# A gated pooling and convolution block on one core: a denser start, with dummy matrix products, wide transposes of the meta tokens and the first block of x in halves

## The chip, the cores and the metric

The kernel runs on one core of a Trainium2 chip. A core has a matrix engine (TensorE, PE in the profile), VectorE (DVE), ScalarE (ACT), GpSimd (POOL) and SyncE (SP). SP, ACT and POOL issue transfers (DMAs) from their own instruction queues, and each engine takes its instructions strictly in their order; an instruction that waits holds up everything behind it on that engine. The metric is the time of one execution on the device in microseconds; the median of several runs counts.

## The reference

One decoder layer over 16 learned meta tokens and 256 tokens of width 2048, in float32:

```python
h = jnp.concatenate([meta_b, x], axis=1)            # 16 + 256 tokens
u = rms_norm(h, g_pre_mix[l])
proj = u @ w_in[l]                                  # 2048 x 7168
z_pool, v_conv, g_conv, gate_a, gate_b = jnp.split(proj, splits, axis=-1)
y_a = causal_multiscale_pool(z_pool, w_pool_grp[l], pool_scale[l]) @ w_pool_out[l]
y_b = conformer_conv(v_conv, g_conv, w_dw[l], b_dw[l], conv_ln_g[l], conv_ln_b[l]) @ w_conv_out[l]
m = jax.nn.sigmoid(gate_a) * y_a + jax.nn.sigmoid(gate_b) * y_b
h = h + rms_norm(m @ w_o[l], g_post_mix[l])
u = rms_norm(h, g_pre_mlp[l])
f = jnp.square(jax.nn.relu(u @ w_up[l])) @ w_down[l]
h = h + rms_norm(f, g_post_mlp[l])
return h[:, N_META:]
```

The split has widths 1024, 1024, 1024, 2048 and 2048; the feed-forward width is 8192.

## The kernel before

Every large product is made of float32 numbers that are split in two parts, hi (rounded to the format fp32r) and lo (the rest), and runs as three products of parts: hi with the activations' hi, hi with their lo, lo with their hi. Weights stream in from memory in chunks of 1 MB, in the order in which they are used (`stream`); SP issues them, ACT casts each chunk to hi (line 250), VectorE subtracts to get lo (line 253), TensorE multiplies. The activations stand with channels on the partitions and tokens along the row (272 of them, the 16 meta tokens first), so x and meta have to be transposed first.

The change lies wholly in the first stage, the first 256 columns of v_conv. There the weights come as two chunks of eight k tiles each (a k tile is 128 input channels), and each k tile is a piece of 128x256 that is cast and split by itself. The order of the work, as it is written by hand (the scheduler is off):

- `make_identity` on GpSimd writes `ident`, the identity with which TensorE transposes.
- The transfers (lines 323 to 334): the meta tokens as 16 rows of 2048 (`m_in`, SP), the gain g_pre_mix (ACT), the first block of x, 512 columns, its lower 128 tokens on SP and its upper 128 on ACT, then the first chunk of weights as pieces of 1, 1, 2, 2 and 2 k tiles (the first on ACT, the rest on SP), block 1 of x (ACT), block 2 (SP), the second chunk, block 3.
- ACT then loads a function table and warms it (`warm_up`, line 286); `keep_warm(8)` puts eight dummy transposes of `ident` on TensorE (line 343).
- `meta_tokens` (lines 351 to 361): sixteen transposes of 16x128 from `m_in`, a transpose of the gain's rows into the columns `vecs` (lines 312 and 313), then VectorE multiplies by the gain (`mg`), ACT casts the hi part into `u`, VectorE makes the lo part. Four more dummies follow.
- `x_tile(k)` (lines 366 to 374): two transposes of 128x128 into one bank, ACT scales by the gain into the hi part of `u`, VectorE makes the lo part.
- The loop over k from -4 to 15: in its first four turns an x tile and a piece of weights each; from k = 0 on the six products of a k tile (`mm3`, line 422: two columns of 128, three products each), and after every odd k the next two x tiles. So the queue of TensorE is: four x tiles, the products of k = 0 and 1, x tiles 4 and 5, the products of k = 2 and 3, and so on.

`m_in` is also read much later, for the sums of squares of the meta tokens (`sq_tile`). `rb` is a tile that is written for the first time near 45 us, with the roots of these sums. Transfers of SP and ACT take one of eight completion semaphores in turn: the ninth transfer takes the first one's and waits, on its own queue, until the first has landed.

Of the kernel before, what the change touches and what calls it, by code (L numbers as in the profile page):

```python
# [8 lines left out]
F32 = mybir.dt.float32  # L9
# [5 lines left out]
P = 128  # L15
CK = 4
CW = 512
# [83 lines left out]
def hybrid_block(ctx: ExitStack, tc: tile.TileContext, ins: dict, out: bass.AP):  # L101
    nc = tc.nc
    x = ins["x"][0]
    meta = ins["meta"]
    T, D = x.shape
    M = meta.shape[0]
    L = M + T
    NT = T // P
    KD = D // P
# [17 lines left out]
    const = ctx.enter_context(tc.tile_pool(name="const", bufs=1))  # L127
# [3 lines left out]
    tmp = ctx.enter_context(tc.tile_pool(name="tmp", bufs=2))  # L131
# [3 lines left out]
    def f32(ap):  # L135
        return ap.bitcast(F32)

    def acc_tile(name):
        return psA.tile([P, CW], F32, tag="acc", name=name)

    def misc_tile(name):
        return psB.tile([P, CW], F32, tag="misc", name=name)
# [43 lines left out]
    HALF = (2 * CK, CW // 2)  # L186
# [24 lines left out]
    opened = []  # L211
# [13 lines left out]
    def part_tile(tag, n, standing=False):  # L225

        key = f"{tag}{n % 3}"
        room = ready.pop(key) if key in ready else part_room(key, f"{tag}_{n}")
        place = 2 if standing and tag == "hi" else 1
        shift = (place - 1 - 3 * KEYS.index(key)) % 4 * LINE  # L230
        return room[:, shift:shift + CK * CW]

    def open_chunk(first=((2, nc.sync),) * 4):
        n = at["n"]
        at["n"] += 1
        src, (rows, width) = stream[n]
        raw = raws.tile([P, CK * CW], F32, tag="raw", name=f"raw_{n}")
        hi, lo = (part_tile(tag, at["parts"], n in standing_chunks) for tag in ("hi", "lo"))
        at["parts"] += 1
        flat, (raw, hi, lo) = raw, (t.rearrange("p (k c) -> p k c", k=rows) for t in (raw, hi, lo))  # L240
        pieces = rows if n < FIRST + 1 else 1
        k = rows // pieces
        i = 0
        for n_, queue in first if n < FIRST else ((rows, nc.sync),):
            sl = slice(i, i + n_)
            queue.dma_start(raw[:, sl, :], src[:, sl, :])
            i += n_

        def high(sl):
            nc.scalar.copy(hi[:, sl, :], raw[:, sl, :])  # L250

        def low(sl):
            nc.vector.tensor_sub(lo[:, sl, :], raw[:, sl, :], f32(hi[:, sl, :]))  # L253

        def piece(i):
            def f():
                sl = slice(i * k, (i + 1) * k)
                high(sl)
                low(sl)
            return f  # L260
        opened.append((hi, lo, [piece(i) for i in range(pieces)], flat))
# [5 lines left out]
    def fetch(ahead=2):  # L267

        for c in range(ahead + 1):
            if c == len(opened) and at["n"] < len(stream):  # L270
                open_chunk()
            if c < len(opened):
                split_pieces(c)
        flush()
        return opened.pop(0)[:2]


    ident = const.tile([P, P], F32, name="ident")
    make_identity(nc, ident)
    ones = const.tile([P, P], F32, name="ones")  # L280
# [9 lines left out]
    m_in = big.tile([M, D], F32, tag="a", name="m_in")  # L290
# [9 lines left out]
    def load_rows(queue, *names):  # L300
        rows = tmp.tile([48, P], F32, tag="g", name=f"rows_{names[0]}")
        n = 0
        for name in names:
            v = ins[name][0].rearrange("(k p) -> k p", p=P)
            queue.dma_start(rows[n:n + v.shape[0], :], v)
            n += v.shape[0]
        return rows, n, names[0]

    def rows_to_columns(rows, n, name):

        pv = misc_tile(f"pv_{name}")
        nc.tensor.transpose(pv[:, :n], rows[:n, :], ident[:n, :n])
        nc.vector.tensor_copy(vecs[:, cols[name]:cols[name] + n], pv[:, :n])
# [1 line left out]
    def col(name, k):  # L315
        return vecs[:, cols[name] + k:cols[name] + k + 1]

    def load_x(queue, b, ts=slice(0, NT)):
        sl = slice(b * CW, (b + 1) * CW)
        queue.dma_start(x_in[:, ts, sl], xv[:, ts, sl])  # L320


    nc.sync.dma_start(m_in, meta)
    pre_rows = load_rows(nc.scalar, "g_pre_mix")
    for t, queue in enumerate((nc.sync, nc.scalar)):
        load_x(queue, 0, slice(t, t + 1))
    open_chunk(((1, nc.scalar), (1, nc.sync), (2, nc.sync), (2, nc.sync), (2, nc.sync)))
    load_x(nc.scalar, 1)
    load_x(nc.sync, 2)
    open_chunk()  # L330
    load_x(nc.sync, 3)
    other_rows = load_rows(nc.gpsimd, "pool_scale", "b_dw", "conv_ln_g", "conv_ln_b", "g_pre_mlp")
# [6 lines left out]
    idle = misc_tile("idle")  # L339

    def keep_warm(n):
        for _ in range(n):
            nc.tensor.transpose(idle[:, :P], ident, ident)

    keep_warm(8)

    u = big.tile([P, KD, 2, -(-L // (4 * LINE)) * 4 * LINE], F32R, tag="um", name="u")[:, :, :, :L]

    def meta_tokens():

        pt = acc_tile("xm")[:, :KD * M].rearrange("p (k m) -> p k m", k=KD)
        for k in range(KD):
            nc.tensor.transpose(pt[:, k, :], m_in[:, k * P:(k + 1) * P], ident[:M, :M])
        rows_to_columns(*pre_rows)
        mg = tmp.tile([P, KD, M], F32, tag="v", bufs=5, name="mg")
        g = vecs[:, cols["g_pre_mix"]:cols["g_pre_mix"] + KD]
        nc.vector.tensor_mul(mg, pt, g[:, :, None].broadcast_to([P, KD, M]))
        nc.scalar.copy(u[:, :, 0, :M], mg)  # L360
        nc.vector.tensor_sub(u[:, :, 1, :M], mg, f32(u[:, :, 0, :M]))

    meta_tokens()
    keep_warm(4)

    def x_tile(k):
        pt = acc_tile(f"xt_{k}")[:, :T]
        sl = slice(k * P, (k + 1) * P)
        for t in range(NT):
            nc.tensor.transpose(pt[:, t * P:(t + 1) * P], x_in[:, t, sl], ident)  # L370
        nc.scalar.activation(u[:, k, 0, M:], pt, AF.Copy, scale=col("g_pre_mix", k))
        nc.vector.scalar_tensor_tensor(
            u[:, k, 1, M:], pt, col("g_pre_mix", k), f32(u[:, k, 0, M:]),
            op0=ALU.mult, op1=ALU.subtract)

    def sq_tile(b, t):
        sl = slice(b * CW, (b + 1) * CW)
        junk = tmp.tile([P, CW], F32, tag="junk", bufs=1, name=f"sqx_{b}_{t}")
        src, n = (x_in[:, t, sl], P) if t < NT else (m_in[:, sl], M)
        nc.scalar.activation(junk[:n, :], src, AF.Square, accum_out=ssq[:n, t, b:b + 1])  # L380
# [6 lines left out]
        nc.vector.tensor_scalar(q, q, -0.5, 1.5, op0=ALU.mult, op1=ALU.add)  # L387
        nc.vector.tensor_mul(r, r, q)

    rb = const.tile([P, L], F32, name="rb")  # L390
    sc = {}

    def scale_roots():
# [23 lines left out]
    def mm3(acc, hi, lo, act, k, cs, first, last):  # L417


        off = act.shape[3] - acc.shape[1]  # L420
        for n, (w, a) in enumerate(((hi, 0), (hi, 1), (lo, 0))):
            nc.tensor.matmul(acc, w[:, k[0], cs], act[:, k[1], a, off:],  # L422
                             start=first and n == 0, stop=last and n == 2)
# [18 lines left out]
    def acc_tiles(name, n=CW // P):  # L442
        return [acc_tile(f"acc_{name}_{j}") for j in range(n)]
# [68 lines left out]
    def pieces_to(n):  # L512

        while first["split"] < min(n, (FIRST + 1) * HALF[0]):
            c = first["split"] // HALF[0]
            if c == at["n"]:
                open_chunk()
            opened[c][2].pop(0)()
            first["split"] += 1

    first = {"split": 0}
    accs = [acc[:, :L] for acc in acc_tiles("v0", HALF_CW // P)]
    squares = [(b, t) for b in range(XB) for t in range(NT + 1)]
    LEAD = 4
    for k in range(-LEAD, KD):
        if k < 0:
            x_tile(k + LEAD)

        pieces_to(min(k + LEAD + 1, KD) + 2 * max(k - KD + LEAD + 1, 0))
        if k < 0:  # L530
            continue
        if k >= HALF[0] and k % 2:
            sq_tile(*squares.pop(0))
        for j, acc in enumerate(accs):
            mm3(acc, *opened[k // HALF[0]][:2], u, (k % HALF[0], k), slice(j * P, (j + 1) * P),
                k == 0, k == KD - 1)
        if k % 2:
            for kx in range(k + LEAD - 1, min(k + LEAD + 1, KD)):
                x_tile(kx)
# [183 lines left out]
    for g in range(NG):  # L723
        for j in range(GK):
            q = g * GK + j
            acc = (acc_tile if q < KP - 2 else misc_tile)(f"acc_grp_{q}")[:, :T]
# [48 lines left out]
    for n in range(NB):  # L775
# [4 lines left out]
    m = big.tile([P, LINE + KD * 2 * T], F32R, tag="um", name="m")[:, LINE:].rearrange(  # L780
        "p (k a t) -> p k a t", k=KD, a=2)
# [421 lines left out]
    accs = acc_tiles("up00")  # L1203
# [498 lines left out]
    for e, cs in enumerate(col_halves):  # L1702
        for w, s in ends:
            h = AT[s][0]
# [47 lines left out]
```

## Time and profile before

| | us |
|---|---|
| median of 3 runs | 1208.12 |
| lowest and highest run | 1207.67, 1209.48 |
| the profiled execution, its own time | 1208.15 |
| its span, first to last instruction | 1206.4 |

The profiled execution stands 0.03 us above the median; its span leaves 1.75 us of its own time outside. The granted clock of TensorE is 0.998 of full speed as a mean. A row of the timeline gives the start and the length in microseconds, the engine (PEld is the loading of weights into TensorE, and a q behind an engine's name is its instruction queue issuing a transfer), the line, the operation, output and inputs, the shape and how many of them were merged into the row; in brackets the idle time ahead of it and what ended that.

### The profile page before, as it was taken

To read this page: it belongs to the slowest core of one execution; us is meant where nothing else is said; L and a number is where in the kernel's file an instruction comes from. 1 tells how busy PE (TensorE), PEld (TensorE's weight loads), DVE (VectorE), ACT (ScalarE), POOL (GpSimd) and SP (SyncE) were. 2 spreads that over 40 slices of the span, in tenths; PEclk is the share of its full clock that TensorE was granted. 3 is DMA by queue.
4 is the path that set the end of the run, shared out by engine and by line. 5 is a ranking of instruction groups with operands and counts; after the bars stand their busy time and mean duration, and the time that the engine had idled before them with its cause. 6 is when DMAs were issued, how large, how long until landed. Compare 5 with 4: busy or idle time off the path is not lost.

```text
span 1206.4 us, 15712 instructions
## 1 busy us (share of the span) xinstructions
PE 1195.8 (99%) x6444; PEld 1038.4 (86%) x6444; DVE 974.7 (81%) x1058; ACT 627.6 (52%) x651; POOL 8.3 (1%) x19
## 2 busy tenths in 40 slices
PE   9999999999999999999999999999999999999997
PEld 9999988888888888898888888888888888888886
DVE  6799978999776778688988878778878778888756
ACT  7533344443583454665555564564554555555542
POOL 1000000000000000000000000000000000000000
PEclk9999999999999999999999999999999999999999
DMA  9655555656558578546475674674764764755841
GB/s 289 210 175 175 178 202 180 208 177 207 175 169 280 176 256 262 181 160 221 144 244 174 187 232 158 198 249 141 245 199 156 261 200 149 244 175 178 275 141 70
DMA packets 162038, 238.27 MB, mean 198 GB/s; under 512 B 4033, under 2 KB 91521, under 8 KB 161440
## 3 DMA queue, kind: packets, MB, share of 16 engines
q1 hardware_dynamic: 159120, 229.98, 58.2%
q0 software_dynamic: 1680, 5.40, 1.7%
q10 hardware_dynamic: 1168, 1.91, 0.4%
q8 instruction: 50, 0.82, 0.3%
q14 instruction: 20, 0.16, 0.0%
HBM read 235.17 MB, written 2.10 MB: 197 GB/s over the span
## 4 chain that ended last, share of the span: by engine, by line
PE 99%; DVE 0%; DMA 0%; DVEq 0%; ACT 0%; issue 0%; ACTq 0%
PE bank_u L427 18%; PE acc_gate L682 14%; PE acc_up L1516 14%; PE bank_u L433 9%; PE bank_a L1516 7%; PE o_c L1020 6%; PE bank_b L1516 5%; PE acc_v L422 4%; PE acc_z L422 4%; PE acc_g L422 4%; PE acc_co L682 4%; PE acc_po L682 4%; PE acc_up L427 1%; PE bank_u L1516 1%; PE o_a L1020 1%; PE acc_up L433 1%
## 5 line engine op out<-in xcount | busy, mean ns | idle before, releaser
L427 PE MATMUL bank_u<-m,hi 128*128 128x512 f32 x960 | 329.9, 390 | 0.0
L433 PE MATMUL bank_u<-m,lo 128*128 128x256 f32 x960 | 265.5, 277 | 0.0
L250 ACT CAST hi<-raw 128x2048 fp32r<-128x2048 f32 (+1 forms) x99 | 151.7, 1548 | 188.9 <-PE acc_gate L682 71.5
L1367 DVE TENSOR_TENSOR lo<-raw_m,hi 128x2048 fp32r<-128x2048 f32 x85 | 194.4, 2289 | 59.2 <-ACT hi L1362 59.2
L1362 ACT CAST hi<-raw_m 128x2048 fp32r<-128x2048 f32 x85 | 162.5, 1912 | 138.1 <-PE bank_u L427 76.8
L253 DVE TENSOR_TENSOR lo<-raw,hi 128x2048 fp32r<-128x2048 f32 (+1 forms) x99 | 180.6, 1835 | 44.1 <-ACT hi L250 43.8
L427 PEld LDWEIGHTS bank_u<-m,hi 128*128 128x128 f32 x960 | 180.2, 188 | 37.9
L433 PEld LDWEIGHTS bank_u<-m,lo 128*128 128x128 f32 x960 | 180.3, 188 | 1.6
L682 PE MATMUL acc_gate<-hi,u 128*128 128x512 f32 x512 | 158.6, 390 | 0.0
L1516 PE MATMUL acc_up<-hi,forms 128*128 128x512 f32 x496 | 157.5, 389 | 0.0
L488 DVE SCALAR_TENSOR_TENSOR c<-a,taps,c 128x256 f32<-128x256 f32 x240 | 115.5, 484 | 7.1 <-ACT c L482 0.5
L682 PEld LDWEIGHTS acc_gate<-hi,u 128*128 128x128 f32 x512 | 96.1, 188 | 20.0
L1516 PEld LDWEIGHTS acc_up<-hi,forms 128*128 128x128 f32 x496 | 93.1, 188 | 19.5
L682 PE MATMUL acc_gate<-lo,u 128*128 128x512 f32 x256 | 99.6, 389 | 0.0
L1516 PE MATMUL acc_up<-lo,forms 128*128 128x512 f32 x248 | 96.6, 389 | 0.0
L1367 DVE TENSOR_TENSOR lo<-raw_c,hi 128x2048 fp32r<-128x2048 f32 x29 | 66.4, 2290 | 21.0 <-ACT hi L1362 21.0
L1516 PE MATMUL bank_a<-hi,forms 128*128 128x512 f32 (+1 forms) x256 | 82.0, 383 | 0.0
L1362 ACT CAST hi<-raw_c 128x2048 fp32r<-128x2048 f32 x29 | 55.3, 1908 | 51.1 <-PE bank_u L427 28.1
L1367 DVE TENSOR_TENSOR lo<-raw_a,hi 128x2048 fp32r<-128x2048 f32 x29 | 66.4, 2289 | 18.4 <-ACT hi L1362 18.4
L1362 ACT CAST hi<-raw_a 128x2048 fp32r<-128x2048 f32 x29 | 55.4, 1910 | 42.4 <-PE bank_u L427 17.1
L1020 PE MATMUL o_c<-hi,m 128*128 128x512 f32 x208 | 65.6, 390 | 0.0
L1516 PE MATMUL bank_b<-hi,forms 128*128 128x512 f32 (+1 forms) x200 | 63.7, 382 | 0.0
(303 smaller groups left out, 1857.1 us busy)
## 6 DMA issues: line engine op xcount, KB each, us to landing
raw<-in_w_in_dram SPq DMA_DIRECT2D x54, 1024.0 KB, 5.1
raw_m<-in_w_down_dram SPq DMA_DIRECT2D x37, 1024.0 KB, 5.3
raw_m<-in_w_up_dram SPq DMA_DIRECT2D x33, 1024.0 KB, 6.2
raw_c<-in_w_down_dram SPq DMA_DIRECT2D x14, 1024.0 KB, 5.3
raw_a<-in_w_up_dram SPq DMA_DIRECT2D x13, 1024.0 KB, 6.0
raw_a<-in_w_down_dram SPq DMA_DIRECT2D x13, 1024.0 KB, 5.2
raw_c<-in_w_up_dram SPq DMA_DIRECT2D x12, 1024.0 KB, 6.0
raw_o<-in_w_o_dram SPq DMA_DIRECT2D x10, 1024.0 KB, 7.5
```

Of the source, the lines that this page charges most:

```text
L250: nc.scalar.copy(hi[:, sl, :], raw[:, sl, :])
L253: nc.vector.tensor_sub(lo[:, sl, :], raw[:, sl, :], f32(hi[:, sl, :]))
L422: nc.tensor.matmul(acc, w[:, k[0], cs], act[:, k[1], a, off:], start=first and n == 0, stop=last and n == 2)
L427: nc.tensor.matmul(acc.rearrange("p (a t) -> p a t", a=2)[:, :, ts], hi[:, k[0], cs], act[:, k[1], :, off + ts.start:off + ts.stop], start ...
L433: nc.tensor.matmul(acc[:, :T], lo[:, k[0], cs], act[:, k[1], 0, off:], start=False, stop=stop, skip_group_check=True)
L488: nc.vector.scalar_tensor_tensor(c, conv["a"][:, q, i:i + T], taps[:, q, i:i + 1], c, op0=ALU.mult, op1=ALU.add)
L682: nc.tensor.matmul(acc, act(kk)[:, a_, ts_], w_[:, k, :], start=kk == 0 and n == 0, stop=kk == nk - 1 and n == 2)
L1020: nc.tensor.matmul(acc, form(k, a_), box[w_][:, k, :], start=start and k == 0 and n == 0, stop=stop and k == CK - 1 and n == 2, skip_group ...
L1362: nc.scalar.copy(box["flat"], raw)
L1367: nc.vector.tensor_sub(lo, raw, f32(box["flat"]))
L1516: nc.tensor.matmul(acc, forms[h][:, f, k, a_, :], box[w_][:, k, cs], start=start and k == 0 and n == 0, stop=stop and k == KH - 1 and n == ...
```

## The change

It has four parts.

1. The dummies become plain products of a tile of ones (`rb`, which is allocated at the start and set to one by VectorE) instead of transposes of `ident`; there are 17 instead of 8 ahead of the meta tokens, and four behind them as before.
2. The meta tokens are loaded a second way, as 256 rows of 128 numbers on 128 partitions (`m_rows`), and turned by two transposes of 128x128; the result stands by token and then by k tile, and is read with the two swapped. `m_in` is still loaded, later.
3. The first block of x comes in halves of its columns: first both token halves' first 256 columns, then, behind the first piece of weights, the rest. Block 1 of x comes in two halves too.
4. The products of k = 0 stand ahead of x tiles 2 and 3 on TensorE.

```diff
         for n_, queue in first if n < FIRST else ((rows, nc.sync),):
+            if n_ == 0:
+                queue()
+                continue
             sl = slice(i, i + n_)
             queue.dma_start(raw[:, sl, :], src[:, sl, :])
...
+    rb = const.tile([P, L], F32, name="rb")
+    nc.vector.memset(rb[:, :P], 1.0)
     ident = const.tile([P, P], F32, name="ident")
...
-    def load_x(queue, b, ts=slice(0, NT)):
-        sl = slice(b * CW, (b + 1) * CW)
+    def load_x(queue, b, ts=slice(0, NT), cs=(0, 2)):
+
+        sl = slice(b * CW + cs[0] * CW // 2, b * CW + cs[1] * CW // 2)
         queue.dma_start(x_in[:, ts, sl], xv[:, ts, sl])
...
+    m_rows = tmp.tile([P, M * KD // P, P], F32, tag="v", bufs=5, name="m_rows")
+    nc.sync.dma_start(m_rows, meta.rearrange("m (k f) -> (m k) f", f=P).rearrange(
+        "(h p) f -> p h f", p=P))
+    pre_rows = load_rows(nc.scalar, "g_pre_mix")
+    load_x(nc.sync, 0, slice(0, 1), (0, 1))
+    load_x(nc.scalar, 0, slice(1, 2), (0, 1))
+
+    def rest_of_block():
+        load_x(nc.sync, 0, slice(0, 1), (1, 2))
+        load_x(nc.scalar, 0, slice(1, 2), (1, 2))
+    open_chunk(((1, nc.scalar), (0, rest_of_block), (1, nc.sync), (2, nc.sync), (2, nc.sync),
+                (2, nc.sync)))
+    load_x(nc.scalar, 1, cs=(0, 1))
+    load_x(nc.scalar, 1, cs=(1, 2))
     nc.sync.dma_start(m_in, meta)
-    pre_rows = load_rows(nc.scalar, "g_pre_mix")
-    for t, queue in enumerate((nc.sync, nc.scalar)):
-        load_x(queue, 0, slice(t, t + 1))
-    open_chunk(((1, nc.scalar), (1, nc.sync), (2, nc.sync), (2, nc.sync), (2, nc.sync)))
-    load_x(nc.scalar, 1)
     load_x(nc.sync, 2)
...
     def keep_warm(n):
         for _ in range(n):
-            nc.tensor.transpose(idle[:, :P], ident, ident)
-
-    keep_warm(8)
+            nc.tensor.matmul(idle[:, :P], rb[:, :P], rb[:, :P], start=True, stop=True)
+
+    keep_warm(17)
...
-        pt = acc_tile("xm")[:, :KD * M].rearrange("p (k m) -> p k m", k=KD)
-        for k in range(KD):
-            nc.tensor.transpose(pt[:, k, :], m_in[:, k * P:(k + 1) * P], ident[:M, :M])
+        pt = acc_tile("xm")[:, :KD * M]
+        for h in range(KD * M // P):
+            nc.tensor.transpose(pt[:, h * P:(h + 1) * P], m_rows[:, h, :], ident)
+        pt = pt.rearrange("p (m k) -> p k m", k=KD)
         rows_to_columns(*pre_rows)
...
+    def product_of(k):
+        for j, acc in enumerate(accs):
+            mm3(acc, *opened[k // HALF[0]][:2], u, (k % HALF[0], k), slice(j * P, (j + 1) * P),
+                k == 0, k == KD - 1)
+
     for k in range(-LEAD, KD):
         if k < 0:
             x_tile(k + LEAD)
 
         pieces_to(min(k + LEAD + 1, KD) + 2 * max(k - KD + LEAD + 1, 0))
+        if k == 1 - LEAD:
+            product_of(0)
         if k < 0:
             continue
         if k >= HALF[0] and k % 2:
             sq_tile(*squares.pop(0))
-        for j, acc in enumerate(accs):
-            mm3(acc, *opened[k // HALF[0]][:2], u, (k % HALF[0], k), slice(j * P, (j + 1) * P),
-                k == 0, k == KD - 1)
+        if k:
+            product_of(k)
```

More of the change, by code (lines that the diff above doesn't have):

```diff
@@ L388, in rsqrt @@
         nc.vector.tensor_mul(r, r, q)
-    rb = const.tile([P, L], F32, name="rb")
     sc = {}
```

## The prediction

> **What bounds the kernel now.** I read the page's busy shares and its chain of waits first, then TensorE's timeline over the first microseconds, then the timelines of the engines that feed it there.
>
> ```profile
> span 1206.4 us, 15712 instructions
> PE 1195.8 (99%) x6444; PEld 1038.4 (86%) x6444; DVE 974.7 (81%) x1058; ACT 627.6 (52%) x651; POOL 8.3 (1%) x19
> PE 99%; DVE 0%; DMA 0%; DVEq 0%; ACT 0%; issue 0%; ACTq 0%
> ```
>
> TensorE bounds the whole span. In the built program all instructions after the first four x tiles and the first product stand in the same order on every engine in both kernels; so what the change is worth is fixed by the moment at which TensorE reaches a common point. I take the fifth x tile (xt 4), which follows the products of k = 0 and 1.
>
> ```profile
> 1.35 1.97 PE L343 MATMUL idle<-ident 128*128 128x128 f32 x8 [1.35 <-POOL ident masks.py:199]
> 3.87 1.89 PE L355 MATMUL xm<-ident,m_in 16*128 16x16 f32 x16 [0.54 <-DMA m_in<-in_meta_dram]
> 5.60 0.26 PE L312 MATMUL pv_g_pre_mix<-ident,rows_g_pre_mix 16*128 16x16 f32 x1
> 5.79 1.11 PE L343 MATMUL idle<-ident 128*128 128x128 f32 x4
> 6.70 1.92 PE L370 MATMUL xt<-ident,x_in 128*128 128x128 f32 x8
> 8.26 0.80 PE L422 MATMUL acc_v<-u,hi 128*128 128x272 f32 x2
> 8.86 0.48 PE L422 MATMUL acc_v<-u,lo 128*128 128x272 f32 x1
> 9.14 0.66 PE L422 MATMUL acc_v<-u,hi 128*128 128x272 f32 x2
> ...
> 10.49 0.42 PE L422 MATMUL acc_v<-u,hi 128*128 128x272 f32 x2
> ...
> 10.88 0.60 PE L370 MATMUL xt<-ident,x_in 128*128 128x128 f32 x4
> ...
> 12.80 0.60 PE L370 MATMUL xt<-ident,x_in 128*128 128x128 f32 x4
> L370 PE MATMUL xt<-ident,x_in x32: 271/272/421, 6.7 to 20.8; 128*128 128x128 f32 x32
> ```
>
> Columns: start, length, engine, line, output and inputs, count; the last row is the x tiles' view with shortest, median and longest in ns. Up to 10.3 us TensorE runs at half speed: eight transposes take 1.97 us, a pitch of (1.97 - 0.42) / 7 = 0.22 us; from 10.88 four take 0.60, a pitch of (0.60 - 0.27) / 3 = 0.11. Two products take 0.66 at 9.14 and 0.42 at 10.49. Between 10.88 and 12.80 lie 4 transposes (0.44) and 12 products, so a fast product takes (1.92 - 0.44) / 12 = 0.123 us. The nearly seven microseconds of transposes from 1.35 to 8.26 did not bring full speed; it came 2.1 us after the first plain product.
>
> ACT and VectorE release the first product:
>
> ```profile
> 2.14 0.46 ACTq L320 DMA_DIRECT2D x_in<-in_x_dram  x1
> 2.63 1.28 ACT L286 ACT_TABLE_LOAD   x1 [2.63 <-issue]
> 3.92 0.20 ACT L286 ACTIVATE warm<-ones 128x1 f32<-128x1 f32 x1
> 6.56 0.40 ACT L360 CAST u<-mg 128x256 fp32r<-128x256 f32 x1 [2.44 <-DVE mg L359]
> 7.37 0.47 ACT L371 ACTIVATE u<-xt,vecs 128x256 fp32r<-128x256 f32 x1 [0.40 <-PE xt L370]
> 7.74 0.39 ACT L250 CAST hi<-raw 128x256 fp32r<-128x256 f32 x1
> 5.90 0.17 DVE L313 COPY vecs<-pv_g_pre_mix 128x16 f32<-128x16 f32 x1 [5.90 <-PE pv_g_pre_mix L312]
> 8.28 0.42 DVE L253 TENSOR_TENSOR lo<-raw,hi 128x256 fp32r<-128x256 f32 x1
> ```
>
> Call U the start of ACT's first x tile (7.37). The first product follows at U + 0.89 (8.26), the third, which wants lo, at U + 1.49 (8.86). xt 4 comes at U + 3.51 (10.88).
>
> **The change part by part.** *The row of dummies.* Twelve transposes become 21 plain f32 products of a tile of ones, 17 ahead of the meta tokens and 4 behind. A plain f32 product costs two passes:
>
> ```profile
> 41.77 1.03 PE L412 MATMUL pb<-diag,ones 16*128 16x16 f32 x6
> 42.56 0.37 PE L422 MATMUL acc_v<-u,hi 128*128 128x272 f32 x1
> 0.73 0.20 POOL masks.py:197 MEMSET ident<- 128x128 f32 x1 [0.29 <-POOLq L1740]
> ```
>
> The kernel issues three pb products and the trace has six, in 42.56 - 41.77 = 0.79 us: 0.13 a pass, close to the transposes' 0.11, which I use for a fast pass, with 0.22 for a slow one. The row needs only VectorE's memset, not GpSimd's identity. VectorE has no row before 5.90, so I take GpSimd's memset: 0.73 + 0.20 + 0.05 = 0.98 us (earliest 0.73; latest the 1.35 of now).
>
> The row's end E depends on W, the slow time before the gate opens. Lower bound 2.1, as after the first product now; upper bound the whole row, 34 x 0.22 = 7.5. I take 3.3, one and a half times the lower bound, because the 2.1 came after transposes that may have counted in part. Then 15 passes are slow and 19 fast: E = 0.98 + 3.3 + 19 x 0.11 = 6.4 us. W = 2.1 gives 5.8, W = 5 gives 7.2.
>
> [...]
>
> *Meta tokens.* Sixteen narrow transposes (1.89 us for 16, on the path now) become two wide ones. From E: two transposes and the gain's one (0.33), eight dummy passes (0.88), then the first x tile, whose second transpose starts 0.11 later and takes 0.27, and 0.03 to ACT: U = E + 1.62. VectorE's and ACT's side is as long: the gain's transpose ends at E + 0.22 + 0.26; from vecs to the cast of u 6.56 - 5.90 = 0.66, the cast 0.40, with 0.04 ahead: E + 1.58. So the four dummies cost nothing as long as this chain covers them; without it they would cost up to 0.9. PE side: U = 8.0.
>
> *ACT's queue.* Eight completion semaphores are handed out in turn, so a ninth transfer waits for the first; the trace has such waits on SP alone so far:
>
> ```profile
> SPq L246 <- DMA rows_g_pre_mix<-in_g_pre_mix_dram: 1.4, 1, 1.4
> m_in<-in_meta_dram SPq DMA_DIRECT2D x1, 128.0 KB, 3.1
> rows_g_pre_mix<-in_g_pre_mix_dram ACTq DMA_DIRECT2D x1, 8.0 KB, 3.3
> x_in<-in_x_dram ACTq DMA_DIRECT2D x1, 256.0 KB, 5.1
> ```
>
> (Second to fourth row: size and us from issue to landing.) The split of x makes more transfers, and now ACT waits: the first half of block 1 for rows_g_pre_mix (issued at 0.73, landed at 4.0), the second half for the first half of block 0's upper tokens. Behind them on ACT stand the table load, the warming of the table, the cast of u and the first x tile. The awaited half, 128 KB, is issued at 1.19 as the second on its queue; it lands 3.1 us later (128 KB first in line) to 5.1 (256 KB second in line), so at 4.3 to 6.3. I take 5.3. Then 0.46 for the issue, 1.28 for the table, 0.20, and 0.40 for the cast: U = 7.6 by ACT, bounds 6.6 and 8.6. The table load that now hides under the wait for x becomes exposed where this side is later than PE's.
>
> *The first product moved ahead of tiles 2 and 3.* From U: third product at U + 1.49, it and three more at the fast pitch, 1.49 + 4 x 0.123 = 1.98; tiles 2 and 3, 0.44; the product of k = 1, 6 x 0.123 = 0.74: xt 4 at U + 3.16. Its hi and lo are ready, since ACT and VectorE took tile 1 right behind tile 0. The pair k = 2 and 3 has tile 2 later than now; its ACT work ends near U + 2.9 and its lo near U + 3.7, against a third product at U + 3.9.
>
> *SP's order.* Pieces 2 and 3 of the weights are issued after the meta rows land (about 4) instead of at 2, pieces 4 and 5 after a half of x (5.3) instead of 4, and the meta tokens are loaded twice (128 KB more), the second time ahead of block 2.
>
> ```profile
> 10.64 0.71 ACT L250 CAST hi<-raw 128x256 fp32r<-128x256 f32 x2 [0.50 <-DMA raw<-in_w_in_dram]
> 13.16 0.50 PE L422 MATMUL acc_v<-u,hi 128*128 128x272 f32 x2
> ```
>
> Pieces 4 and 5 land at 10.6 now, and their first product runs at 13.16: 2.5 us of cover, which outlasts a transfer issued 1.3 later. I charge nothing; uncovered, up to 1.3 us less what the smaller load ahead of them gives back.
>
> *The sum.* U = max(8.0, 7.6) = 8.0, xt 4 at 8.0 + 3.16 = 11.2 against 10.88: 0.3 us later. Against the profiled execution's 1208.15 us (span 1206.4 and 1.75 around it; the median is 1208.12, so no shift): 1208.4 us. The early halves, the faster clock and the saved transposes are nearly all spent in waiting for a longer row. With the bounds: W = 2.1 and an early half give U = 7.4 and xt 4 at 10.6, -0.3; W = 5 gives U = 8.8 and 12.0, +1.1.
>
> **The rivals.** *It does what it says:* the gate opens early, so that the row ends when the meta rows land (4.0), and ACT's side sets U. For it: m_in landed 3.1 us after its issue, and everything behind it is short. Against: 34 passes even at 0.11 take 3.7 us, from 0.98 to 4.7, and ACT's lower bound is 6.6. Then xt 4 at 6.6 + 3.16 = 9.8, -1.1: 1207.0 us.
>
> *ACT's table load sets U:* the half lands as late as a whole one does now (6.3). For it: the DMA engines are shared by as many bytes. Against: fewer bytes stand ahead. U = 8.6, xt 4 at 11.8, +0.9: 1209.0 us.
>
> *Slower, the gate stays shut:* two-pass f32 products are counted no more than the transposes, which have the same pitch in the rows and opened nothing in seven microseconds. Against: the first plain products, though single passes, opened it in 2.1. Then E = 0.98 + 7.5 = 8.5; the same steps at 0.22 give U = 8.5 + 3 x 0.22 + 8 x 0.22 + 0.22 + 0.45 = 11.6; the first product at 12.5, four slow ones after 13.1 (0.9), four transposes (0.9), and six fast products (0.74): xt 4 at 15.6, +4.8: 1212.9 us. It decides from E = 8.5 with a fast chain behind it, where xt 4 is 2.4 later.
>
> **How the numbers follow.** Forecast 0.50, does what it says 0.25, ACT's table load 0.13, gate shut 0.10, anything else 0.02. Faster or slower counts from 0.2% (2.4 us), about what a measurement of this kernel can tell from no change. The first three all lie within it: 0.88, less 0.03 for noise. Slower: 0.12 (gate shut, and some of that noise). Faster 0.03: even the best case gains 1.1. The range reaches below the -1.1 and above the +1.1 by the half-width of the three runs shown (1207.67 to 1209.48), and leaves out the shut gate: 1207.0 - 0.9 = 1206.1 and 1209.25 + 0.9 = 1210.2.
>
> **What would show it.** In TensorE's timeline: 17 dummies as 34 passes from about 1.0 us, a pitch that falls from 0.22 to 0.11 within the row, the meta transposes at 6.4 and the first product near 8.9 at the fast pitch; in ACT's, the table load at about 5.8 instead of 2.63, after a DMA that waited; xt 4 near 11.2. The row is wrong if the pitch stays 0.22 to its end, ACT's term if the table load still starts before 4, and the forecast if xt 4 comes before 10 or after 13, or if the pairs of k behind it take more than 1.92 us.

## The result: 2 us slower, and the profile after

| | before | after |
|---|---|---|
| median of 22 runs | 1208.17 | 1210.17 |
| lowest and highest run | 1207.65, 1210.26 | 1209.36, 1210.62 |
| the profiled execution, its own time | 1208.15 | 1209.36 |
| its span | 1206.4 | 1207.6 |

The ratio is 1.0014, with a 95% interval of 1.0008 to 1.0021: slower by 0.14%, still inside the 0.2% that counted as no change in the prediction, but 2.0 us where 0.3 were forecast. The profiled execution is the lowest of the 22, so the trace explains 1.2 us (1209.36 - 1208.15) and says nothing direct of the other 0.8. The page of after, busy times and chain by engine:

```profile
span 1207.6 us, 15753 instructions
PE 1196.8 (99%) x6460; PEld 1039.5 (86%) x6460; DVE 974.7 (81%) x1059; ACT 627.7 (52%) x651; POOL 8.3 (1%) x19
PE 99%; DVE 0%; ACT 0%; DVEq 0%; issue 0%; ACTq 0%
```

TensorE still bounds the span, and the page shows no more. Its timeline in after, at the start:

```profile
1.05 5.84 PE L359 MATMUL idle<-rb 128*128 128x128 f32 x34 [1.05 <-DVE rb L282]
6.73 0.38 PE L371 MATMUL xm<-ident,m_rows 128*128 128x128 f32 x2
7.04 0.23 PE L317 MATMUL pv_g_pre_mix<-ident,rows_g_pre_mix 16*128 16x16 f32 x1
7.20 1.16 PE L359 MATMUL idle<-rb 128*128 128x128 f32 x8
8.20 0.60 PE L387 MATMUL xt<-ident,x_in 128*128 128x128 f32 x4
9.44 0.62 PE L438 MATMUL acc_v<-u,hi 128*128 128x272 f32 x2 [0.64 <-ACT hi L253]
...
11.79 0.60 PE L387 MATMUL xt<-ident,x_in 128*128 128x128 f32 x4
...
13.75 0.60 PE L387 MATMUL xt<-ident,x_in 128*128 128x128 f32 x4
```

The 17 dummies are 34 passes and hold TensorE until 6.73; xt 4, the yardstick of the sum, comes at 11.79 against 10.88 before, 0.91 later. The full clock came within the row: the trace's clock record has it at 4.80 (10.47 before), and xt 4 to xt 6 take 1.96 us. ACT and VectorE on the same stretch, in two timelines of after:

```profile
2.22 2.44 ACTq L326 DMA_DIRECT2D x_in<-in_x_dram  x3
4.70 1.28 ACT L291 ACT_TABLE_LOAD   x1 [4.70 <-DMA x_in<-in_x_dram]
5.99 0.20 ACT L291 ACTIVATE warm<-ones 128x1 f32<-128x1 f32 x1
7.98 0.41 ACT L377 CAST u<-mg 128x256 fp32r<-128x256 f32 x1 [1.79 <-DVE mg L376]
8.62 0.47 ACT L388 ACTIVATE u<-xt,vecs 128x256 fp32r<-128x256 f32 x1 [0.23 <-PE xt L387]
```

```profile
7.31 0.17 DVE L318 COPY vecs<-pv_g_pre_mix 128x16 f32<-128x16 f32 x1 [6.31 <-PE pv_g_pre_mix L317]
```

ACT did wait for its second semaphore: in after's trace the first transfers of SP and ACT use eight semaphores, the first half of block 1 of x was issued at 2.75, when the gain had landed (2.73) whose semaphore it takes, and the second at 4.28, when the half of x had (4.26). The table load, behind them, moved from 2.63 to 4.70; but it then idled 1.79 us for VectorE, which had waited 6.31 us for TensorE. Nothing but the row of dummies, and the short steps on TensorE behind it, stands ahead of the first product. The chain of waits over the first 45 us, by line, of before and then of after, says the same:

```profile
by line: PE acc_v L422 46.7%; PE acc_g L422 26.3%; PE xt L370 9.6%; DMA m_in<-in_meta_dram 6.9%; PE xm L355 4.2%; PE idle L343 2.3%; PE pb L412 2.1%; issue 0.2%; PE pv_g_pre_mix L312 0.2%
```

```profile
by line: PE acc_v L438 43.8%; PE acc_g L438 26.3%; PE idle L359 15.4%; PE xt L387 7.3%; PE pb L428 2.1%; ACT u L388 1.1%; ACT hi L253 0.7%; PE xm L371 0.5%; issue 0.5%; DVE rb L282 0.4%; PE pv_g_pre_mix L317 0.4%
```

Before, the chain began with a load of 3.1 us (6.9%) and sixteen transposes; after, the dummies alone are 15.4% of 45 us, 6.9 us.

The lag stays almost as it is to the end. The last matmul and the last transfers that SP issues, of before and then of after:

```profile
1197.39 0.28 PE L1516 MATMUL bank_b<-hi,forms 128*128 128x256 f32 x1
...
1202.13 1.12 SPq L1680 DMA_DIRECT2D out_dram<-raw_m  x2
```

```profile
1198.22 0.28 PE L1539 MATMUL bank_b<-hi,forms 128*128 128x256 f32 x1
...
1202.97 1.12 SPq L1703 DMA_DIRECT2D out_dram<-raw_m  x2
```

TensorE ends 0.83 us late and the transfers are issued 0.84 late. But the span ends 1.2 late: from the start of the last matmul to the end it is 9.35 us instead of 8.99. So the 1.2 us of the profiled execution are 0.84 from the start of the kernel and 0.36 from its very end, where no instruction of the kernel was changed. The range of the prediction ended at 1210.2, so the median lies 0.03 us inside it.

### The profile page after: what moved, and what is told of

Read it like the earlier page. It is cut to its first block, busy times and chain, and to the rows that moved or that the text cites. A ratio compares the mean times of both kernels' runs of the same rounds, so it can differ in the third digit from the quotient of the medians.

```text
span 1207.6 us, 15753 instructions
## 1 busy us (share of the span) xinstructions
PE 1196.8 (99%) x6460; PEld 1039.5 (86%) x6460; DVE 974.7 (81%) x1059; ACT 627.7 (52%) x651; POOL 8.3 (1%) x19
## 4 chain that ended last, share of the span: by engine, by line
PE 99%; DVE 0%; ACT 0%; DVEq 0%; issue 0%; ACTq 0%
PE bank_u L443 18%; PE acc_gate L705 14%; PE acc_up L1539 14%; PE bank_u L449 9%; PE bank_a L1539 7%; PE o_c L1043 6%; PE bank_b L1539 5%; PE acc_v L438 4%; PE acc_z L438 4%; PE acc_g L438 4%; PE acc_co L705 4%; PE acc_po L705 4%; PE acc_up L443 1%; PE bank_u L1539 1%; PE o_a L1043 1%; PE acc_up L449 1%
```

## The experiments

Two theories. *The row*: 17 dummies last to 6.7 us although half of x has landed by 4.3, so a shorter row gives the time back. *The stream*: the meta tokens are now loaded twice, and the transfers of x and of the weights, which keep the DMA engines busy from about 6 us on (a share of 0.95 and more in each microsecond to 9), come later by that. Their rival: the second wait of ACT, or the number of transfers to issue. All kernels were timed in five rounds beside the kernel before, which had 1208.10 to 1208.25. "Shift" is how much later an instruction of TensorE starts than the same one before.

### Shorter rows, no row, transposes instead

The changed kernel with 8 dummies in place of 17:

```diff
-    keep_warm(17)
+    keep_warm(8)
```

> The changed kernel with 8 products ahead of the meta tokens instead of 17. Row theory (the row of dummies is longer than the wait for the data, and everything behind it is late): the row's 16 slow passes of 0.22 us end at 4.6 us instead of 6.7, ACT's side (table load over at 6.2, cast of u 0.4) sets its first x tile at 6.6 to 6.8, the fifth x tile comes near 10.0 instead of 11.8, the time is 1207.5 to 1208.4 us. Transfer theory (the new transfers and ACT's waits for them set the start): ACT's first x tile stays near 8.6 and the time within 0.4 us of the changed kernel's 1210.2.

1209.70 us (1209.28 to 1210.37), ratio 1.0011 [1.0002, 1.002]. TensorE's timeline:

```profile
1.05 3.76 PE L359 MATMUL idle<-rb 128*128 128x128 f32 x16 [1.05 <-DVE rb L282]
4.63 0.40 PE L371 MATMUL xm<-ident,m_rows 128*128 128x128 f32 x2
...
7.36 0.62 PE L438 MATMUL acc_v<-u,hi 128*128 128x272 f32 x2 [0.64 <-ACT hi L253]
...
10.10 0.63 PE L387 MATMUL xt<-ident,x_in 128*128 128x128 f32 x4 [0.23 <-DMA x_in<-in_x_dram]
...
12.81 0.63 PE L387 MATMUL xt<-ident,x_in 128*128 128x128 f32 x4 [0.59 <-DMA x_in<-in_x_dram]
...
15.69 0.52 PE L387 MATMUL xt<-ident,x_in 128*128 128x128 f32 x3 [0.73 <-DMA x_in<-in_x_dram]
```

The row theory held for the first product, 2.1 us earlier than in after (7.36 against 9.44), and missed the time: from xt 4 on, x tiles wait for transfers of x. The shift goes from -0.91 at the first product over 0.00 at xt 6 to +1.46 at xt 12. A gain of 0.9 against before became a loss of 1.4.

Without any dummies:

```diff
-    keep_warm(17)
...
-    keep_warm(4)
```

> The changed kernel with no dummy at all. Row theory: ACT's first x tile at 6.6 us, the first product near 7.5 at half speed, the gate open 2 to 4 us later, the fifth x tile at 10.3 to 11.0; 1207.7 to 1208.8 us, so better than with 17. If instead the open gate is what the row buys and is worth more than it costs: over 1210.2 us. Transfer theory: near 1210.2 or more.

1210.05 us (1209.68 to 1211.27), ratio 1.0015 [1.0006, 1.0024]. The first product starts at 7.32, at half speed; the clock rose at 12.2. The shift is +0.95 near 19 us and +1.61 at the end. So the changed kernel is as slow without a row as with its row of 17.

With the transposes of before as dummies, 8 and 4:

```diff
-            nc.tensor.matmul(idle[:, :P], rb[:, :P], rb[:, :P], start=True, stop=True)
+            nc.tensor.transpose(idle[:, :P], ident, ident)
...
-    keep_warm(17)
+    keep_warm(8)
```

> The changed kernel with the dummies of before (8 and 4 transposes of the identity), so everything but the row. Row theory: ACT's first x tile at 6.6 to 6.8 us, half speed until 2 us behind the first product, the fifth x tile at 10.1 to 10.6: 1207.4 to 1208.2 us. Transfer theory: the loss stays, 1210 us.

1209.95 us (1209.03 to 1210.41), ratio 1.0011 [1.0002, 1.002]. First product at 7.63, shift -0.63; then +0.31 at 10.5, +0.86 at 31 and +1.43 at the products with the diagonal near 42 us. Between 12 and 30 us the shift stays near +0.4; what follows is a short wait for weights at 30.9 and one near 43 that before did not have:

```profile
43.20 1.00 PE L428 MATMUL pb<-diag,ones 16*128 16x16 f32 x6 [0.39 <-DVE diag L422]
```

The diagonal needs the sums of squares of x, and ACT takes these among its casts of the weights. The kernel without dummies waits 0.59 us at the same place. That late weights are what delays the sums is argued from the order of ACT's work, not tested. Three starts with three rows, all 1.4 to 1.8 us over before: the row is not the only bound.

### The row alone, in the kernel before

The kernel before with the row of 17 and 4 plain products and no transfer changed:

```diff
+    rb = const.tile([P, L], F32, name="rb")
+    nc.vector.memset(rb[:, :P], 1.0)
...
-            nc.tensor.transpose(idle[:, :P], ident, ident)
-    keep_warm(8)
+            nc.tensor.matmul(idle[:, :P], rb[:, :P], rb[:, :P], start=True, stop=True)
+    keep_warm(17)
```

> The kernel before with the row alone: 17 and 4 plain products of ones instead of 8 and 4 transposes, nothing else changed. Row theory: the row ends at 6.7 us, sixteen narrow transposes follow (1 us or more), ACT's first x tile is at 9.2 or later and the fifth x tile at 12.5 or later: 1210 to 1211.5 us. Transfer theory: no transfer is changed, so no loss: 1207.5 to 1208.4.

1209.84 us (1209.1 to 1210.76), ratio 1.0012 [1.0003, 1.0021].

```profile
1.05 6.97 PE L345 MATMUL idle<-rb 128*128 128x128 f32 x34 [1.05 <-DVE rb L279]
7.96 1.16 PE L357 MATMUL xm<-ident,m_in 16*128 16x16 f32 x16
...
11.35 0.62 PE L423 MATMUL acc_v<-u,hi 128*128 128x272 f32 x2 [0.20 <-ACT hi L250]
```

In this execution (1210.54 us) the clock rose only at 7.19, and the same 34 passes took 6.97 us instead of 5.84. What the row delays stays delayed: the shift is +2.35 to +2.46 from xt 4 to the end. The median is 0.7 under this execution, so most runs probably had a shorter row.

The same with 6 and 2 products, and with 9 and 2:

```diff
-    keep_warm(17)
+    keep_warm(6)       # the other kernel: 9
...
-    keep_warm(4)
+    keep_warm(2)
```

> The kernel before with plain products as dummies, 6 ahead of the meta tokens and 2 behind (24 and 8 slow passes' worth of nothing but 12 and 4 passes), no transfer changed. Gate theory (plain products open the gate early, and that is the one part of the change that pays): the row ends at 3.7 us when the meta tokens land, the clock is full between 5 and 8 us instead of 10.5, the fifth x tile comes at 9.8 to 10.5 instead of 10.9: 1207.2 to 1207.9 us. If the stream of transfers bounds the kernel before as well: 1208.2.

> The kernel before, all transfers as they were, with 9 plain products ahead of the meta tokens and 2 behind instead of transposes. Gate theory: 18 passes of 0.22 us from 1.05 end at 5.0, the clock is full between 4.7 and 8.3 us, ACT's first x tile stays near 7.4, the fifth x tile comes at 10.2 (bound by block 1 of x, landed at 10.2) instead of 10.9: 1207.3 to 1207.9 us. If the row does not open the gate (as with 6, where the clock was full at 10.1): 1208.2 or, with the row's 1.1 us on the path, 1209.

With 6: 1208.20 us (1207.69 to 1208.68), ratio 1.0 [0.9991, 1.0009]. That row ended at 3.8, the clock rose at 10.15, and nothing moved; so the tile of ones and its memset cost nothing. With 9: 1208.72 us (1207.83 to 1210.25), ratio 1.0004 [0.9995, 1.0013]. The clock rose at 3.89, and the first product came 0.46 early, but TensorE then stopped:

```profile
7.80 0.62 PE L423 MATMUL acc_v<-u,hi 128*128 128x272 f32 x2 [0.20 <-ACT hi L250]
...
10.80 0.63 PE L372 MATMUL xt<-ident,x_in 128*128 128x128 f32 x4 [0.94 <-DMA x_in<-in_x_dram]
```

xt 4 comes at 10.80 against 10.88 before. Block 1 of x, which it wants, landed at 10.7 here; in the trace of before it had landed by 10.2 (issued at 2.14, 8.1 us). So with the transfers of before some 0.7 us could be gained at xt 4 at the best, and here it was 0.1.

### Where the second load lies

The load of `m_in` moved behind block 3 of x, with a row of 17 and with a row of 8:

```diff
-    nc.sync.dma_start(m_in, meta)
     load_x(nc.sync, 2)
     open_chunk()
     load_x(nc.sync, 3)
+    nc.sync.dma_start(m_in, meta)
```

> The changed kernel (row of 17) with the second load of the meta tokens (16 rows of 8 KB) moved from ahead of block 2 of x to behind block 3. Two bounds theory (the row delays TensorE, and behind it this load, whose 8 KB packets take 0.55 to 0.67 us, slows the stream of x and weights between 8 and 13 us): the row still ends near 6.9 us or later, so the fifth x tile stays at 11.8 to 12.5 us; the bytes moved by 12 us rise from 2.7 MB to 3.0 or more; the time falls a little, to 1209.2 to 1209.9. Row theory alone: no change, 1210.2. Issue theory (what starves the stream is the waiting of SP and ACT for semaphores, not this load): no change in bytes, 1210.2.

> As the run before with a row of 8 instead of 17. Two bounds theory: both bounds gone; TensorE's waits for x of 0.23 and 0.59 us that the row of 8 alone showed at 10 and 12.8 us shrink to under 0.3 in all, the shift against the kernel before, which grew from -0.9 to +1.4 there, stays below 0: 1207.4 to 1208.4 us, against 1209.7 with the row of 8 alone. Issue theory: the waits stay, 1209.4 to 1209.9.

Row 17: 1210.24 us (1209.51 to 1210.97), ratio 1.0017 [1.0008, 1.0026]. Row 8: 1210.33 us (1209.54 to 1211.08), ratio 1.0017 [1.0008, 1.0026]. Neither gained, where 0.3 to 1.0 and 1.3 to 2.3 us were expected: behind block 3 the load is no better hidden. What was moved shows in the windows (start and end, length, busy time of the engines, granted clock, share of the DMA engines, GB/s in the last column; the clock's column counts the time ahead of the clock record's first entry as full speed). Before, after, and the moved load with a row of 8:

```profile
10.00:12.00 2.00, 2.00 (x17) 2.00 (x16) 1.80 (x6) 1.50 (x5) 0.00 (x0) 1.00 1.05 368
12.00:14.00 2.00, 2.00 (x19) 2.00 (x18) 1.62 (x5) 1.51 (x6) 0.00 (x0) 1.00 1.07 345
```

```profile
10.00:12.00 2.00, 2.00 (x17) 2.00 (x17) 1.15 (x4) 1.04 (x4) 0.00 (x0) 1.00 1.07 215
12.00:14.00 2.00, 2.00 (x19) 2.00 (x18) 2.00 (x7) 2.00 (x8) 0.00 (x0) 1.00 1.03 293
...
16.00:18.00 2.00, 2.00 (x20) 2.00 (x18) 2.00 (x6) 1.54 (x5) 0.00 (x0) 1.00 1.07 371
```

```profile
10.00:12.00 2.00, 2.00 (x19) 2.00 (x18) 2.00 (x6) 2.00 (x7) 0.00 (x0) 1.00 1.06 347
...
16.00:18.00 2.00, 1.67 (x14) 1.45 (x12) 2.00 (x6) 2.00 (x6) 0.00 (x0) 1.00 1.10 195
18.00:20.00 2.00, 1.21 (x10) 1.24 (x11) 0.30 (x2) 0.82 (x4) 0.00 (x0) 1.00 1.06 265
```

The engines of the DMA are busy throughout (a share above 1 counts overlapping packets), but where the load lies they move 195 to 215 GB/s instead of 345 to 371. The dip moved from 10 to 14 us to 16 to 20 us along with the load. TensorE's timeline with the moved load and the row of 8 has one longer wait in place of the three at 10 to 16 us:

```profile
18.80 0.63 PE L387 MATMUL xt<-ident,x_in 128*128 128x128 f32 x4 [1.13 <-DMA x_in<-in_x_dram]
```

That wait takes the shift from -1.07 to +0.21. The rest comes between 24 and 44 us in smaller waits, the longest 0.50 for weights at 31.9 and 0.38 at the diagonal at 44.1, and TensorE ends 2.4 us late. The loss of rate went along with the load; its place in the order decides only what waits.

### The rival: ACT's wait, and the number of transfers

Row of 8, and block 1 of x in one transfer, so that ACT waits once:

```diff
-    load_x(nc.scalar, 1, cs=(0, 1))
-    load_x(nc.scalar, 1, cs=(1, 2))
+    load_x(nc.scalar, 1)
```

> The row of 8 with block 1 of x in one transfer, so that ACT waits for one landing (the gain, 2.7 us) instead of two; the second load of the meta tokens stays ahead of block 2. Issue theory: the table load starts near 3.2 instead of 4.7 us, SP and ACT keep more in flight, the bytes moved by 12 us rise to 3.0 MB, 1208.4 us or less. Two bounds theory: the table load moves as said, but the stream is as slow at 9 to 13 us and TensorE waits for x as before: 1209.3 to 1209.9.

1210.74 us (1209.97 to 1211.3), ratio 1.0021 [1.0012, 1.003], the slowest of all. ACT was free as expected:

```profile
2.22 0.95 ACTq L326 DMA_DIRECT2D x_in<-in_x_dram  x2
3.20 1.28 ACT L291 ACT_TABLE_LOAD   x1 [3.20 <-DMA rows_g_pre_mix<-in_g_pre_mix_dram]
```

The table load came 1.5 us earlier and bought nothing; the first product came at 7.71, and x tiles waited again. The bytes moved by 12 us did not rise to 3.0 MB (2.68, with the row of 8 2.63). The theory of ACT's wait falls. Up to 30 us this kernel is ahead of the row of 8 (+0.95 against +1.50); it loses 1.5 us behind that, most of it in a wait of 0.50 for weights at 31.7 and one of 0.64 at the diagonal at 44.2. Why it waits there and the row of 8 doesn't stays open.

### Without the second load

Row of 8, and no second load; then the row of 17 and no second load:

```diff
-    nc.sync.dma_start(m_in, meta)
...
+    nc.gpsimd.memset(m_in, 1.0)
...
-    keep_warm(17)      # the first kernel alone
+    keep_warm(8)
```

> The changed kernel with a row of 8 and without the second load of the meta tokens (GpSimd sets that tile to ones instead, so the sums of squares of the meta tokens are left out). Second load theory (its sixteen 8 KB packets slow the whole stream wherever it is full: 0.2 to 0.25 MB per us around them instead of 0.36, at 9 to 13 us in the changed kernel and at 17 to 20 us when it was moved back): the third chunk of weights lands at 21.0 to 22.0 us (22.9 with the row of 8, 23.9 with the load moved back, 21.1 in the kernel before), the fourth at 24 to 25, TensorE's shift against the kernel before stays between -1.0 and 0.0 us up to 46 us: 1207.4 to 1208.3 us. Small transfers theory (halves of x and fewer bytes in flight cost the stream its rate): third chunk still near 22.7, 1209.2 or more.

> The changed kernel with its row of 17 dummies, without the second load of the meta tokens (their rows for the sums of squares are set to ones by GpSimd, so those sums are left out). Two bounds of which the later one counts (the row of dummies first, the stream of transfers later): the row alone still starts the first product near 9.4 us (before: 8.26) and TensorE stays 0.9 to 1.2 us behind the kernel before from there to the end; with the 0.37 us of the longer tail the median is 1209.3 to 1210.0, above the 1208.5 of the same kernel with a row of 8. If the second load alone costs the time, a short and a long row come to the same 1208.2 to 1208.7. If the two costs add up, this kernel lies as far under the changed kernel's 1210.17 as the row of 8 without the load lies under the row of 8 with it (1209.7 - 1208.5 = 1.2): 1209.0.

Row 8: 1208.52 us (1207.94 to 1208.85), ratio 1.0002 [0.9993, 1.0011]. TensorE's timeline in it, and two windows of the row of 8 with the load (first) and without it:

```profile
1.06 3.74 PE L359 MATMUL idle<-rb 128*128 128x128 f32 x16 [1.06 <-DVE rb L282]
...
7.34 0.62 PE L438 MATMUL acc_v<-u,hi 128*128 128x272 f32 x2 [0.64 <-ACT hi L253]
...
9.70 0.60 PE L387 MATMUL xt<-ident,x_in 128*128 128x128 f32 x4
...
11.65 0.60 PE L387 MATMUL xt<-ident,x_in 128*128 128x128 f32 x4
```

```profile
10.00:12.00 2.00, 1.90 (x16) 1.93 (x16) 1.83 (x6) 1.99 (x7) 0.00 (x0) 1.00 1.07 185
12.00:14.00 2.00, 1.41 (x12) 1.22 (x11) 0.82 (x3) 0.57 (x2) 0.00 (x0) 1.00 1.05 285
```

```profile
10.00:12.00 2.00, 2.00 (x19) 2.00 (x18) 2.00 (x7) 1.97 (x7) 0.00 (x0) 1.00 1.05 360
12.00:14.00 2.00, 2.00 (x20) 2.00 (x18) 1.89 (x6) 1.34 (x5) 0.00 (x0) 1.00 1.10 352
```

No wait for x of over 0.2 us, no dip; xt 4 comes 1.18 us before that of the kernel before, and TensorE ends 0.81 early. This kernel differs from the first experiment in the load and in what goes with it (a memset on GpSimd in its place, one transfer fewer in the turn of the semaphores). The number of transfers is not what counts: with the load moved it stayed the same, and the dip moved along. So the load costs 1.2 us in the medians, 1209.70 to 1208.52. The two traces have 2.2 us at TensorE's end (+1.38 to -0.81), but the second is the fastest execution of its 11.

Row 17: 1210.07 us (1209.74 to 1210.72), ratio 1.0017 [1.0008, 1.0026].

```profile
1.06 6.16 PE L359 MATMUL idle<-rb 128*128 128x128 f32 x34 [1.06 <-DVE rb L282]
...
9.76 0.62 PE L438 MATMUL acc_v<-u,hi 128*128 128x272 f32 x2 [0.64 <-ACT hi L253]
```

| medians, us | row of 17 | row of 8 |
|---|---|---|
| second load on SP | 1210.17 | 1209.70 |
| no second load | 1210.07 | 1208.52 |

If the two costs added up, the gains of removing each alone (0.47 and 0.10) would give 1209.60 with both removed; it is 1208.52. They are two bounds, of which the later one counts: with the row of 17 the load hides behind the row, with the row of 8 the row hides behind the load. Only with both gone the time can't be told from that of before. The kernels in the second line of the table carry a cost of their own: in their runs 1.88 to 2.05 us of the time lie outside the span, in those of the first line 1.73 to 1.83, which makes them some 0.17 us dearer without any instruction of the kernel. The three kernels with the load elsewhere have that too; why is open.

The load put first on GpSimd's queue, with a row of 8:

```diff
     rb = const.tile([P, L], F32, name="rb")
     nc.vector.memset(rb[:, :P], 1.0)
+    x_in = big.tile([P, NT, D], F32, tag="k8", bufs=2, name="x_in")
+    m_in = big.tile([M, D], F32, tag="a", name="m_in")
+    nc.gpsimd.dma_start(m_in, meta)
     ident = const.tile([P, P], F32, name="ident")
...
-    x_in = big.tile([P, NT, D], F32, tag="k8", bufs=2, name="x_in")
-    m_in = big.tile([M, D], F32, tag="a", name="m_in")
...
-    nc.sync.dma_start(m_in, meta)
...
-    keep_warm(17)
+    keep_warm(8)
```

> The changed kernel with a row of 8 and the second load of the meta tokens issued first of all, on GpSimd's queue, where little else is in flight. Second load theory: the stream loses only the 128 KB (0.35 us), the first halves of x land 0.1 to 0.5 us later, the third chunk lands at 21.5 to 22.3 us, TensorE's shift stays between -0.8 and 0.4: 1207.6 to 1208.6 us. Small transfers theory: as the row of 8 alone, 1209.3 to 1210.

1209.45 us (1208.95 to 1211.64), ratio 1.0014 [1.0005, 1.0023]; the profiled execution, its lowest, took 1208.95. The load ran at 3.3 to 4.9 us, and so delayed the first halves of x, which landed at 5.2 and 5.4 instead of 4.1 and 4.3; the first product came at 8.32, and TensorE ended 0.19 late. Between 10 and 14 us there is no dip (1.44 MB moved, 0.94 with the load on SP). Better in the trace, not clearly in the medians, and 0.85 us over what the second load theory gave at most. No version is faster than the kernel before.

## Why the prediction was right in direction and short in size

- **TensorE's start, the two passes.** The row starts at 1.05 (0.98 said), as 34 passes. The passes have the pitch that was said: by their single starts 0.213 us slow (0.22 said) and 0.112 fast (0.11). Only the first pass of a row is longer, which the sum left out: 0.375 us at half speed, 0.214 at full speed.
- **The gate.** It opened 3.75 us into the row, where 3.3 was taken. The rival with the gate shut fell, and with it the idea that two-pass products count as little as transposes: with transposes the clock rose at 10.99, with the row at 4.80. So E is 6.73, 0.36 later than the 6.37 of the sum: the row started 0.07 later, its 17 slow passes took 3.78 us instead of 3.3, and its 17 fast ones 1.90 instead of 2.09 for 19. U, at 8.62, is E + 1.89 and not E + 1.62: the meta tokens and the gain took 7.20 - 6.73 = 0.47 instead of 0.33, and the eight dummies behind them 1.00 instead of 0.88, for their long first pass. The steps were right; this term is 0.6 too small.
- **From U to xt 4.** 3.17 measured, 3.16 said, but in this two misses cancel: tiles 2 and 3 took 0.36 (0.44 said), the product of k = 1 0.84 (0.74). The first pair behind takes 1.96, which is over the 1.92 that was named as a sign against the forecast; the next ones take 1.92 to 1.94, and the lag only grows from 0.91 to 0.97.
- **ACT's queue.** It waited as said, but the table load started at 4.70 (5.8 said), since a half of x landed sooner, some 3.0 us after its issue. It was not the bound, and freeing it bought nothing. The rival of the table load fell.
- **SP's order: "I charge nothing".** In the changed kernel that is what it cost, 0.10 us between the medians with and without the load. But the reason given, 2.5 us of cover at pieces 4 and 5, was not the one that counted: the cover was the long row. The prediction priced the load by its place in the queue (1.3 us at most), not by what it does to the rate of the transfers behind it. With a row of 8 it cost 1.2 us of the median.
- **The rival "does what it says".** Its xt 4 (9.8, 1.1 early) was met by the row of 8 without the load (9.70). Its price was not: TensorE ends 0.81 early, the end of the kernel takes back 0.4, another 0.2 lies outside the span (1.96 us against 1.77), and the median is 1208.52, not 1207.0. That kernel's profiled execution, 1207.94, is its lowest; the medians show no gain.
- **What the sum lacked.** The end of the kernel, 0.36 us: in all ten kernels with the changed transfers the span ends 9.34 to 9.45 us after the start of the last matmul, in the four with the transfers of before 8.99 to 9.02. About 0.1 of it lies between the last issue and its landing (2.67 against 2.56), the rest after the last landing, where the profile shows no instruction: 0.89 to 0.90 us with the transfers of before, 1.13 to 1.14 with four more on SP and ACT, 1.19 to 1.20 with three more. Why is open, and wasn't tried.
- **One execution for the median.** The sum was made against one profiled execution, and after's is the lowest of 22. The other 0.8 us can't be read from a trace here. A row whose gate opens later is one candidate: the same 34 passes took 5.84, 5.90, 6.16 and 6.97 us in four kernels, and each microsecond of a later gate makes the row 1 - 0.112 / 0.213 = 0.47 longer. But 0.8 asks for a gate that opens 1.7 us later, 5.4 into the row, and of the ten openings listed below only one came so late. A late wait at the diagonal is another: in after it was ready at 42.47 and its products started at 42.73, and in the kernel with the row of 17 and the load moved, whose profiled execution (1210.14) is near its median, TensorE waited 0.36 us for it. Neither was shown.

So of the 2.0 us, 0.3 was forecast, 0.6 is the mis-sized row with the steps behind it, 0.36 the end, and 0.8 stands outside the trace. That the median still lies in the range is luck: neither the end nor the 0.8 stood in the sum, and the range reached to 1210.2 only by the 0.9 that was added for the spread of three runs. The sentence that held best is the one on where the gains go: they are spent in waiting for a longer row.

## What to carry to other kernels

A row that warms the clock has to end when the first data land: here 34 passes lasted to 6.7 us for data that had landed by 4.3, and a clock that is fast early gains no more than the transfers allow: with the row of 9 TensorE stopped for block 1 of x until 10.80, and the median gained nothing. Price an added transfer by the rate of all that follows it, and look for the dip in GB/s at an unchanged busy share (10 to 12 us: 215 GB/s at a share of 1.07 in after, 368 at 1.05 before); moved behind block 3, the load here only took the dip along, to 16 to 20 us (195 and 265 GB/s). When one of two such costs is removed and the time hardly moves, remove both before calling either harmless.

## What the runs showed of the hardware

**One small load slows the whole stream.** The second load of the meta tokens is 128 KB in 16 packets of 8 KB, one to each of 16 partitions. Packets in the trace of after, by microsecond of their start (size, count, mean ns), with the kernel without the load at the end:

```
 8 us: 1 KB  x235: 59
10 us: 1 KB  x103: 88    2 KB x23: 174    8 KB x8: 674
11 us: 1 KB   x37: 87    2 KB x73: 145    8 KB x3: 556
13 us: 1 KB  x215: 50    2 KB x63: 93
without the load
11 us: 1 KB  x164: 48    2 KB x98: 89
```

While it runs, the other packets take 1.6 to 1.9 times as long. Between 10 and 14 us, the row of 8 with the load moved 0.94 MB (185 and 285 GB/s), the one without 1.42 (360 and 352): 0.48 MB less, for a load of 0.13. The same data as 256 rows of 512 bytes on 128 partitions, at the very start, landed 2.2 us after its issue; as 16 rows, also at the start, it took 3.1 before. The packets of 8 KB took 0.55 to 0.67 us as means in each microsecond, so a wait for one such packet is less than the time by which the weights behind it came late: the first chunk of eight k tiles behind block 3 landed at 22.9 with it and at 20.8 without, row of 8 in both. Whether the size of the packets does it, or that all 16 go to the same 16 of the 128 partitions, no run here separates.

**The opening of the gate spreads widely.** From the start of an unbroken row of plain products at 1.05, the clock rose after 2.84, 3.56, 3.60, 3.70, 3.75, 3.90, 3.90, 4.43, 4.52 and 6.14 us in the ten traces of such rows (a row of 8 has ended after 3.58, so most of its openings fall just behind it); a row of 12 passes that ended at 3.8 did not open it at all. The earliest and the latest lie 3.3 us apart. In all 14 traces the stretch at full speed has one of three lengths, 3.41 us apart from one to the next: 1191.25 us in before is the shortest and 1198.08 in after the longest, 349 and 351 times 3.4133. The rows start at 1.05 or 1.06 us in all ten, and openings that spread over nearly one such step would fit a clock that changes in steps of 3.41 us; that was not tested.
